# Seven block products in place of eight in the first feed-forward product, from the second quarter on

## The chip, the cores and the metric

The kernel runs on one core of one Trainium2 chip, in one launch. The metric is the device time of one execution in microseconds (us). A core has engines that each work through their own list of instructions in order and wait for each other by semaphores: TensorE (PE) for matrix products, VectorE (DVE) and ScalarE (ACT) for elementwise work, GpSimd (POOL), and SyncE (SP), which here only issues DMA transfers. Matrix products write to PSUM; everything else lives in SBUF. On TensorE each product is preceded by the load of its 128x128 stationary operand (PEld in the profile), which overlaps the product before it.

## The reference

One decoder layer on 256 tokens of width 2048, in float32. The part that matters here is the end of it, `x = x + merged @ w_out` and after that the feed-forward block:

```
def _rms(x, g):
    x32 = x.astype(jnp.float32)
    y = x32 * lax.rsqrt(jnp.mean(x32 * x32, axis=-1, keepdims=True) + EPS)
    return (y * g.astype(jnp.float32)).astype(x.dtype)
...
        h2 = _rms(x, g_ffn_norm[layer])
        x = x + jnp.square(jax.nn.relu(h2 @ w_ff_in[layer])) @ w_ff_out[layer]
```

`w_ff_in` is 2048 x 8192 and `w_ff_out` 8192 x 2048. Ahead of this lie three token mixers with their projections, gates and up-projections, which the change does not touch.

## The kernel before

**Products.** Every weight matrix is read from memory once, in float32, in tiles of two 128-row blocks by 512 columns (512 KB). Each tile lands in a buffer `raw` by a DMA that SP issues, is split by ACT into a rounded part `whi` (L159, L232) and by DVE into the rest `wlo` (L160, L233), and is used by TensorE for three products per 128-row block and token half: `whi` with the high and the low part of the activations, `wlo` with the high part. So a tile costs 2 token halves x 3 x 2 = 12 products of 512 columns. `wahead` (L200) keeps three tiles loaded and split ahead of the one in use; four buffers each hold `whi` and `wlo` (pool `wp`, L81), eight hold `raw` during the feed-forward block (pool `wff`, L700).

**Two ways to multiply.** `strip_rows` (L211) computes 256 tokens by 512 columns over 16 row blocks: 8 tiles, 96 products. `unit` (L238) computes 256 x 1024, that is two such strips. On the first four row blocks it treats the product as 2x2 blocks times 2x2 blocks and uses seven block products in place of eight, each with 6 matmuls: `B11`, `T2`, `T3`, `T1`, `B21`, `T4`, `B22`. The sums of weight blocks (`T1` to `T4`) are made by DVE in `uload` (L165) from four raw tiles that are loaded together, the sums of activation blocks by `sums_of` (L707, tiles `sf` and `ss`). The other 12 tiles of a unit are plain, marked `n`. A list of names, `UNIT`, says in which order products and plain tiles follow. Four of the block products go to PSUM tiles of their own (`pp`), and once they are done `early` adds them up on DVE (`uu`, `wz`) into what each output tile still lacks; `late` adds the accumulators `acc` at the unit's end.

**The feed-forward block.** It runs in four quarters (`for q in range(4)`, L741) of 2048 hidden columns. A quarter is four strips of `w_ff_in` with `strip_rows`, whose results are multiplied by the row scale of the norm (`ss2`, an ACT operand), put through relu and square (L724, L725), transposed by TensorE (L733) and split (`hid`), and then two units of `w_ff_out`. The norm's row scale is applied to the result of the first product, not to its input: the transposed activations `x1T` hold x times the gain alone. DVE and POOL compute `ss2` (L693 to L695).

**What sets the order.** The program is written as a loop over tiles. After each tile `pump` (L116) takes one step of pending work (transposes, splits, sums) from the queue `posts`, and one from `attn`. A scheduler then orders each engine's list from this program; the lists are fixed before the run.

Of the kernel before, what the change touches and what calls it, by code (L numbers as in the profile page):

```python
# [18 lines left out]
P = 128  # L19
# [21 lines left out]
GA = 2  # L41


UNIT = ["B11", "T2", "n", "T3", "n", "T1", "n", "B21", "n", "T4", "n", "B22", "n", "n", "n", "n", "n", "n", "n"]
UNIT_BLOCKS = [(0, 0), (1, 1), (0, 1), (1, 0)] + [(kg, c) for kg in range(2, KT // GA) for c in range(2)]


# [29 lines left out]
def tile_block(ctx: ExitStack, tc: tile.TileContext, io):  # L77
# [52 lines left out]
    for c in range(4):  # L130
        for name, nk in (("w_up_a", AH), ("w_up_b", BH), ("w_up_c", CH)):
            plan.extend([(name, GA, 512)] * (nk // GA))
        plan.extend([("w_gate", GA, 512)] * (min(3, 8 - 3 * c) * KT // GA))
    plan.extend([("w_out", GA, 512)] * (4 * KT // GA))
    for q in range(4):
        plan.extend([("w_ff_in", GA, 512)] * (4 * KT // GA))
        for _ in range(2):
            plan.extend((("w_ff_out", k) if k != "n" else ("w_ff_out", GA, 512)) for k in UNIT)
    offs = {}
    last_load = [None]  # L140
    pool = [wp]
# [534 lines left out]
    for c in range(4):  # L676
        acc = strip_rows("w_out", 512, KT, mh, ml)
        cs = slice(c * 512, (c + 1) * 512)
        for t in range(2):
            nc.vector.tensor_tensor(x1[:, t, cs], acc[t], x1[:, t, cs], op=ALU.add)  # L680
            sq = ff.tile([P, 512], F32, tag="sq2", name="sq2", bufs=2)
            nc.scalar.activation(sq, x1[:, t, cs], AF.Square, accum_out=stat2[:, t, c:c + 1])
        for j in range(2):
            tp = ps_tp.tile([P, 2, S], F32, tag="tp", name="tp")
            for i in range(2):
                kt = 4 * c + 2 * j + i
                for t in range(2):
                    nc.tensor.transpose(tp[:, i, t * P:(t + 1) * P], x1[:, t, kt * P:(kt + 1) * P], ident)  # L688
            for i in range(2):
                kt = 4 * c + 2 * j + i  # L690
                split_into(x1T[:, kt, 0, :], x1T[:, kt, 1, :], tp[:, i, :], vcol(V_FFN + kt))
# [12 lines left out]

    S_USE = {"T1": 0, "T2": 1, "T3": 2, "B22": 3}

    def sums_of(tps, ss):  # L707

        (a11, a12), (a21, a22) = [[tp[:, 2 * i:2 * i + 2, :] for i in range(2)] for tp in tps]
# [9 lines left out]
    def hidden_post(acc, hh, ss):  # L719

        ys = []
        for t in range(2):
            y = ff.tile([P, 512], F32, tag="y", name="y", bufs=4)
            nc.scalar.activation(y, acc[t], AF.Relu, scale=ss2[:, t:t + 1])  # L724
            nc.scalar.activation(y, y, AF.Square)  # L725
            ys.append(y)
        yield
        tps = []
        for t in range(2):
            yield  # L730
            tp = ps_tp.tile([P, 4, P], F32, tag="tp", name="tp")
            for i in range(4):
                nc.tensor.transpose(tp[:, i, :], ys[t][:, i * P:(i + 1) * P], ident)  # L733
            ts = slice(t * P, (t + 1) * P)
            split_into(hh[:, :, 0, ts], hh[:, :, 1, ts], tp)
            tps.append(tp)
        if ss is not None:
            yield
            sums_of(tps, ss)

    for q in range(4):  # L741
        hid = []
        for sidx in range(4):
            if sidx == 1:
                pool[0] = wff
            acc = strip_rows("w_ff_in", 512, KT, x1h, x1l)
            hh = ff.tile([P, 4, 2, S], F32R, tag="hid", name="hid", bufs=5)
            if sidx == 0:
                ss = ff.tile([P, 2, 4, 2, P], F32R, tag="ss", name="ss", bufs=1)
            gen = hidden_post(acc, hh, ss if sidx == 0 else None)  # L750
            next(gen)
            posts.append(("h", gen))
            hid.append(hh)
        hidh = lambda kt, t: hid[kt // 4][:, kt % 4, 0, t * P:(t + 1) * P]
        hidl = lambda kt, t: hid[kt // 4][:, kt % 4, 1, t * P:(t + 1) * P]
        h0 = hid[0]
        sums = {k: (lambda hl, g, i=i: ss[:, hl, i, g, :]) for k, i in S_USE.items()}
        sums["B11"] = lambda hl, g: h0[:, g, hl, 0:P]
        sums["B21"] = lambda hl, g: h0[:, GA + g, hl, 0:P]
        sums["T4"] = lambda hl, g: h0[:, GA + g, hl, P:S]  # L760
        for u in range(2):
            cols = [slice(1024 * u + 512 * c, 1024 * u + 512 * (c + 1)) for c in range(2)]

            def early(p1, p6, p7, p5):
                uu = ff.tile([P, 2, 512], F32, tag="uu", name="uu", bufs=1)
                wz = ff.tile([P, 2, 512], F32, tag="wz", name="wz", bufs=1)
                nc.scalar.copy(uu[:, 0, :], p1)
                nc.vector.tensor_tensor(x1[:, 0, cols[0]], p1, x1[:, 0, cols[0]], op=ALU.add)
                nc.vector.tensor_tensor(uu[:, 0, :], p6, uu[:, 0, :], op=ALU.add)
                nc.vector.tensor_tensor(uu[:, 1, :], p7, uu[:, 0, :], op=ALU.add)  # L770
                nc.vector.tensor_tensor(wz, p5[:, None, :].to_broadcast([P, 2, 512]), uu, op=ALU.add)
                nc.vector.tensor_tensor(x1[:, 1, cols[0]], uu[:, 1, :], x1[:, 1, cols[0]], op=ALU.add)
# [7 lines left out]
            unit("w_ff_out", sums, hidh, hidl, early, late)  # L780


def _consts():
# [62 lines left out]
```

## Time and profile before

| | |
|---|---|
| time, median of 3 runs | 1416.14 us (1415.92 to 1416.81) |
| the profiled execution's own time | 1416.98 us |
| its span | 1415.2 us |
| PE busy | 1405.5 us, 99% of the span |
| PEld busy | 1163.8 us, 82% |
| DVE busy | 890.1 us, 63% |
| ACT busy | 709.6 us, 50% |
| POOL busy | 36.6 us, 3% |
| memory read | 271.31 MB, 193 GB/s over the span |

The span runs from the first to the last instruction that the profiler saw; 1.78 us of the profiled execution's own time lie outside it. PE's busy time counts a product from its start to its modelled end, and products overlap: what a product costs in a row of products is the distance of their starts, which is total time by count.

### The profile page before, as it was taken

The numbers are of one execution on the slowest core, as the hardware profiler recorded it, in microseconds if no ns is written. First come the engines' busy times: TensorE is split into PE (matmuls) and PEld (weight loads), VectorE is DVE, ScalarE is ACT, GpSimd is POOL, SyncE is SP. The second block draws the span as 40 slices with busy tenths as digits, with TensorE's granted clock in tenths as the row PEclk, the third lists the DMA queues.
The fourth block names the chain that finished last, engine by engine and source line by source line (L and its number), as shares of the span: only waits on it lengthen the run. The fifth ranks groups of instructions, "written<-read, shape, count | busy, mean of one in ns | idle before, by whom it ended". The sixth has DMA issues, their size and how long they took to land.

```text
span 1415.2 us, 17005 instructions
## 1 busy us (share of the span) xinstructions
PE 1405.5 (99%) x6408; PEld 1163.8 (82%) x6408; DVE 890.1 (63%) x987; ACT 709.6 (50%) x881; POOL 36.6 (3%) x41
## 2 busy tenths in 40 slices
PE   8999999999999999999999999999999999999998
PEld 6888888888888888888888888888888888888887
DVE  6647657556655646565555786557865578655785
ACT  7545545465444444445455544455444554455542
POOL 0211102000000000000000000000000000000000
PEclk9999999999999999999999999999999999999999
DMA  9747545655566666676666557664676645766562
GB/s 320 238 143 238 169 149 164 200 180 169 185 202 200 196 201 207 193 241 191 185 247 184 155 184 248 189 186 149 195 240 190 185 155 194 239 185 187 155 229 92
DMA packets 79265, 274.51 MB, mean 194 GB/s; under 512 B 9040, under 2 KB 9808, under 8 KB 78928
## 3 DMA queue, kind: packets, MB, share of 16 engines
q1 hardware_dynamic: 79040, 273.42, 61.7%
q8 instruction: 50, 0.82, 0.2%
q14 instruction: 31, 0.25, 0.0%
q10 hardware_dynamic: 144, 0.02, 0.0%
HBM read 271.31 MB, written 2.10 MB: 193 GB/s over the span
## 4 chain that ended last, share of the span: by engine, by line
PE 74%; DVE 0%; issue 0%
PE acc L222 48%; PE acc L256 21%; PE pp L256 3%; PE tp L733 1%; PE tp L660 0%; PE tp L688 0%; DVE x L776 0%
## 5 line engine op out<-in xcount | busy, mean ns | idle before, releaser
L160 DVE TENSOR_TENSOR wlo<-raw,whi 128x1024 fp32r<-128x1024 f32 (+2 forms) x471 | 568.1, 1208 | 423.5 <-ACT whi L159 419.7
L159 ACT CAST whi<-raw 128x1024 fp32r<-128x1024 f32 (+2 forms) x471 | 489.2, 1040 | 576.8 <-PE acc L222 392.5
L222 PE MATMUL acc<-whi,xT 128*128 128x512 f32 (+1 forms) x1472 | 394.1, 389 | 5.3 <-ACT xT L235 5.3
L222 PEld LDWEIGHTS acc<-whi,xT 128*128 128x128 f32 x1472 | 273.1, 189 | 60.8 <-ACT xT L235 6.0
L222 PE MATMUL acc<-whi,x1T 128*128 128x512 f32 x1024 | 277.3, 392 | 0.0
L222 PE MATMUL acc<-wlo,xT 128*128 128x512 f32 (+1 forms) x736 | 227.1, 389 | 0.0
L256 PE MATMUL acc<-whi,hid 128*128 128x512 f32 x832 | 222.3, 390 | 0.0
L222 PEld LDWEIGHTS acc<-whi,x1T 128*128 128x128 f32 x1024 | 190.4, 188 | 38.6
L256 PEld LDWEIGHTS acc<-whi,hid 128*128 128x128 f32 x832 | 155.9, 188 | 32.4
L222 PEld LDWEIGHTS acc<-wlo,xT 128*128 128x128 f32 x736 | 137.3, 189 | 28.4 <-issue 1.0
L222 PE MATMUL acc<-wlo,x1T 128*128 128x512 f32 x512 | 157.8, 389 | 0.0
L256 PE MATMUL acc<-wlo,hid 128*128 128x512 f32 x416 | 125.3, 390 | 0.0
L222 PEld LDWEIGHTS acc<-wlo,x1T 128*128 128x128 f32 x512 | 96.1, 188 | 20.5
L256 PEld LDWEIGHTS acc<-wlo,hid 128*128 128x128 f32 x416 | 77.8, 188 | 16.0
L233 DVE TENSOR_TENSOR wlo<-raw,whi 128x1024 fp32r<-128x1024 f32 x56 | 68.3, 1220 | 27.0 <-ACT whi L232 21.3
L232 ACT CAST whi<-raw 128x1024 fp32r<-128x1024 f32 x56 | 58.9, 1053 | 45.1 <-PE acc L256 26.3
L222 PE MATMUL acc<-whi,mT 128*128 128x512 f32 x256 | 69.9, 391 | 0.0
L222 PE MATMUL acc<-whi,oT 128*128 128x512 f32 x224 | 60.0, 390 | 0.6 <-ACT oT L235 0.6
L222 PEld LDWEIGHTS acc<-whi,mT 128*128 128x128 f32 x256 | 47.8, 188 | 9.6
L222 PEld LDWEIGHTS acc<-whi,oT 128*128 128x128 f32 x224 | 42.0, 188 | 9.6 <-ACT oT L235 0.9
L222 PE MATMUL acc<-wlo,mT 128*128 128x512 f32 x128 | 40.0, 391 | 0.0
L222 PE MATMUL acc<-wlo,oT 128*128 128x512 f32 x112 | 34.8, 390 | 0.0
(160 smaller groups left out, 811.5 us busy)
## 6 DMA issues: line engine op xcount, KB each, us to landing
raw<-in_w_ff_in_dram SPq DMA_DIRECT2D x128, 512.0 KB, 3.9
raw<-in_w_ff_out_dram SPq DMA_DIRECT2D x128, 512.0 KB, 4.2
raw<-in_w_gate_dram SPq DMA_DIRECT2D x96, 512.0 KB, 3.6
raw<-in_w_proj_dram SPq DMA_DIRECT2D x77, 512.0 KB, 3.8
raw<-in_w_out_dram SPq DMA_DIRECT2D x32, 512.0 KB, 3.6
raw<-in_w_up_c_dram SPq DMA_DIRECT2D x12, 512.0 KB, 3.5
raw<-in_w_up_a_dram SPq DMA_DIRECT2D x8, 512.0 KB, 3.5
raw<-in_w_up_b_dram SPq DMA_DIRECT2D x8, 512.0 KB, 3.5
```

What stands on the lines that cost most here:

```text
L159: nc.scalar.copy(hi[:, gs, :], raw[:, gs, :])
L160: nc.vector.tensor_tensor(lo[:, gs, :], raw[:, gs, :], hi[:, gs, :].bitcast(F32), op=ALU.subtract)
L222: nc.tensor.matmul(acc[t][:, :n], lhsT=xs(kt, t), rhs=ws[:, g, :], start=(first and kt == 0), stop=(last and kt == nkt - 1),)
L232: nc.scalar.copy(hi, src)
L233: nc.vector.tensor_tensor(lo, src, hi.bitcast(F32), op=ALU.subtract)
L256: nc.tensor.matmul(acc, lhsT=x(hl, g), rhs=w[:, g, :], start=(first and i == 0 and g == 0), stop=(last and i == 2 and g == GA - 1))
L733: nc.tensor.transpose(tp[:, i, :], ys[t][:, i * P:(i + 1) * P], ident)
```

## The change

From the second quarter on, `w_ff_in` is multiplied by `unit` too: two units in place of four strips. The first quarter keeps its strips.

- The relu of a unit's result has no accumulator to read at once, since the block products must be added first. `late` now adds on DVE (L814 of the new code) into `y`, and relu and square run on ACT without a scale.
- So the scale must be in the activations. `scale_rows` spreads the row scale over a 128 x 256 tile `rrow` with two float32 products of a matrix of ones with a diagonal matrix `dg`, then rebuilds the activations in float32 (`xs`, four tiles of 128x1024 in the old weight buffers) and multiplies them by `rrow`. This runs on the side of the first quarter's strips.
- `split_rows` splits `xs` back into `x1T` when the first quarter's strips are done with it, and makes the activation sums for the block products (`sx`) once for all six new units.
- The list `UNIT` has two plain tiles more between `T2` and `T3`, and two fewer at its end, for old and new units alike.
- `early` and `partial_sums`: the copy of the first block product gets a tile of its own (`p1s`). `sq2` shares the buffers of `y`. The buffer reserved for software DMA descriptors is made smaller. The host's layout of `w_ff_in` follows the units.

```diff
-UNIT = ["B11", "T2", "n", "T3", "n", "T1", "n", "B21", "n", "T4", "n", "B22", "n", "n", "n", "n", "n", "n", "n"]
+UNIT = ["B11", "T2", "n", "n", "n", "T3", "n", "T1", "n", "B21", "n", "T4", "n", "B22", "n", "n", "n", "n", "n"]
...
+    def scale_rows():
+        tp = ps_sc.tile([P, S], F32, tag="sc", name="rr")
+        for t in range(2):
+            dg = ff.tile([P, P], F32, tag="a21", name="dg", bufs=1)
+            nc.vector.tensor_scalar(dg, ident, ss2[:, t:t + 1], None, op0=ALU.mult)
+            nc.tensor.matmul(tp[:, t * P:(t + 1) * P], lhsT=tri[:, P:], rhs=dg, start=True, stop=True)
+        nc.scalar.copy(rrow, tp)
+        for g in range(0, KT, 4):
+            yield
+            f = wp.tile([P, 4, S], F32, tag="raw", name="xs")
+            nc.vector.tensor_tensor(f, x1T[:, g:g + 4, 0, :].bitcast(F32), x1T[:, g:g + 4, 1, :].bitcast(F32),
+                                    op=ALU.add)
+            yield
+            nc.vector.tensor_tensor(f, f, rrow[:, None, :].to_broadcast([P, 4, S]), op=ALU.mult)
+            scaled.append(f)
+
+    def split_rows():
+        yield
+        for g, f in enumerate(scaled):
+            yield
+            split_into(x1T[:, 4 * g:4 * g + 4, 0, :], x1T[:, 4 * g:4 * g + 4, 1, :], f)
+            if g == 0:
+                yield
+                sums_of([[f[:, 2 * j:2 * j + 2, i * P:(i + 1) * P] for j in range(2)] for i in range(2)], sx)
...
-        for sidx in range(4):
+        for sidx in range(4 if q == 0 else 0):
             if sidx == 1:
                 pool[0] = wff
+                attn.append(("x", scale_rows()))
             acc = strip_rows("w_ff_in", 512, KT, x1h, x1l)
...
+        for u in range(2 if q else 0):
+            more = {}
+
+            def early(*p):
+                more[0, 0], more[0, 1], wz = partial_sums(*p)
+                more[1, 0], more[1, 1] = wz[:, 0, :], wz[:, 1, :]
+
+            def late(c, t, acc):
+                y = ff.tile([P, 512], F32, tag="y", name="y", bufs=4)
+                nc.vector.tensor_tensor(y, acc, more[c, t], op=ALU.add)
+                nc.scalar.activation(y, y, AF.Relu)
+                nc.scalar.activation(y, y, AF.Square)
+                more["y", t] = y
+                if t:
+                    first = u == 0 and c == 0
+                    posts.append(("h", hidden_rows([more["y", 0], y], hid[2 * u + c], ss if first else None,
+                                                   0 if c else 2)))
+
+            unit("w_ff_in", sums_for(lambda kt, hl, ts: x1T[:, kt, hl, ts], sx), x1h, x1l, early, late)
+        if q == 0:
+            drain(attn, "x")
+            attn.append(("x", split_rows()))
```

What this does to the engines' lists shows at three places. The first is TensorE in the second quarter's `w_ff_in`, where a strip had one kind of row: `acc` from `x1T`, here with the transposes of an earlier strip's `y` between.

```order
L222 MATMUL acc<-whi,x1T 128x512 x4
L222 MATMUL acc<-wlo,x1T 128x512 x2
L733 MATMUL tp<-ident,y 128x128 x4
L222 MATMUL acc<-whi,x1T 128x512 x4
L222 MATMUL acc<-wlo,x1T 128x512 x2
```

Now a new unit (its second in the quarter) begins with two block products of six matmuls each, `B11` from `x1T` and `T2` from the sums `sx`, and the transposes of the unit before follow at once.

```order
L262 MATMUL pp<-whi,x1T 128x512 x4
L262 MATMUL pp<-wlo,x1T 128x512 x2
L262 MATMUL pp<-whi,sx 128x512 x4
L262 MATMUL pp<-wlo,sx 128x512 x2
L262 MATMUL acc<-whi,x1T 128x512 x4
L752 MATMUL tp<-ident,y 128x128 x4
L262 MATMUL acc<-wlo,x1T 128x512 x2
```

The kinds of rows are those that a `w_ff_out` unit had before, with other operands.

The second place is VectorE at the head of that same new unit. There the splits of the coming weights (`wlo`) now stand between the splits of `hid` and the sums `sf` and `ss`.

```order
L738 TENSOR_TENSOR uu<-pp,p1s 128x512
L239 TENSOR_TENSOR wlo<-raw,whi 128x1024
L239 TENSOR_TENSOR hid<-tp,hid 128x4x128
L166 TENSOR_TENSOR wlo<-raw,whi 128x1024
L239 TENSOR_TENSOR hid<-tp,hid 128x4x128
L239 TENSOR_TENSOR wlo<-raw,whi 128x1024
L719 TENSOR_TENSOR sf<-tp,a21s 128x256
L720 TENSOR_TENSOR sf<-tp,a21s 128x256
L721 SCALAR_TENSOR_TENSOR sf<-tp,sf 128x256
L722 TENSOR_TENSOR sf<-tp,sf 128x256
L166 TENSOR_TENSOR wlo<-raw,whi 128x1024
L239 TENSOR_TENSOR ss<-sf,ss 128x1024
```

Before, the same sums stood among the splits of a strip, as here in the second quarter, where nothing else is pending.

```order
L233 TENSOR_TENSOR hid<-tp,hid 128x4x128
L160 TENSOR_TENSOR wlo<-raw,whi 128x1024
L233 TENSOR_TENSOR hid<-tp,hid 128x4x128
L713 TENSOR_TENSOR sf<-tp,a21s 128x256
L714 TENSOR_TENSOR sf<-tp,a21s 128x256
L715 SCALAR_TENSOR_TENSOR sf<-tp,sf 128x256
L160 TENSOR_TENSOR wlo<-raw,whi 128x1024
L716 TENSOR_TENSOR sf<-tp,sf 128x256
L160 TENSOR_TENSOR wlo<-raw,whi 128x1024
L233 TENSOR_TENSOR ss<-sf,ss 128x1024
```

So the sums moved from a strip, with one split per plain tile, into a unit, whose block products need a split every six matmuls.

The third place is VectorE in the first and second strip of the first quarter. Here are the rows of the change, from the first `xs` on; before, there were only `wlo` rows.

```order
L775 TENSOR_TENSOR xs<-x1T 128x1024
L166 TENSOR_TENSOR wlo<-raw,whi 128x1024
L775 TENSOR_TENSOR xs<-x1T 128x1024
L166 TENSOR_TENSOR wlo<-raw,whi 128x1024 x2
L775 TENSOR_TENSOR xs<-x1T 128x1024
L769 TENSOR_SCALAR dg<-ident,ss_95 128x128
L166 TENSOR_TENSOR wlo<-raw,whi 128x1024 x3
L778 TENSOR_TENSOR xs<-xs,rrow 128x1024 x4
L166 TENSOR_TENSOR wlo<-raw,whi 128x1024
L239 TENSOR_TENSOR hid<-tp,hid 128x4x128
```

The second `dg` stands behind the last `xs` addition, and the four multiplications by `rrow` stand in one piece between two weight splits.

On TensorE the second product from `dg` stands in the middle of the second strip's third tile, so TensorE's list holds there until `dg` is written.

```order
L228 MATMUL acc<-whi,x1T 128x512 x4
L770 MATMUL rr<-dg,tri 128x128
L228 MATMUL acc<-wlo,x1T 128x512 x2
```

Before, the two `L228` rows followed each other without it.

## Rows read from the trace of the kernel before

**Rows 1.** The page's busy time of each engine: us, share of span, instructions.

```profile
PE 1405.5 (99%) x6408; PEld 1163.8 (82%) x6408; DVE 890.1 (63%) x987; ACT 709.6 (50%) x881; POOL 36.6 (3%) x41
```

**Rows 2.** Whole run, whom PE waited for: us in total, times, longest us.

```profile
PE acc L222 <- ACT xT L235: 5.3, 2, 4.9
PE acc L222 <- ACT oT L235: 0.6, 1, 0.6
```

**Rows 3.** Chain of waits, second quarter: start us, us, what, count.

```profile
885.39 27.20 PE acc L222 x120
912.59 0.44 PE tp L733 x4
913.03 2.78 PE acc L222 x12
...
975.40 2.72 PE pp L256 x12
...
991.35 27.20 PE acc L256 x120
1018.55 2.72 PE pp L256 x12
...
1060.71 0.45 PE acc L222 x2
```

**Rows 4.** Busy us (and count) of PE, PEld, DVE, ACT, POOL by stretch; clock, DMA share, GB/s.

```profile
800.07:843.23 43.16, 43.16 (x196) 35.70 (x195) 34.19 (x34) 22.51 (x26) 0.00 (x0) 1.00 0.62 195
843.23:885.39 42.16, 42.16 (x188) 34.91 (x187) 30.31 (x30) 20.43 (x21) 0.00 (x0) 1.00 0.74 237
885.39:975.40 90.01, 90.01 (x410) 74.42 (x409) 50.62 (x48) 45.99 (x55) 0.00 (x0) 1.00 0.56 170
885.39:1060.71 175.32, 175.32 (x790) 145.03 (x789) 115.13 (x111) 88.92 (x99) 0.00 (x0) 1.00 0.62 192
```

**Rows 5.** PE timeline at float32 products of 128 columns: start us, us, what, records.

```profile
197.13 0.39 PE L564 MATMUL pn<-tri,nfb 128*128 128x128 f32 x2
197.35 0.60 PE L563 MATMUL pn<-tri,nfb 128*128 128x256 f32 x2
```

**Rows 6.** DVE timeline, head of the first quarter's second unit.

```profile
841.99 1.21 DVE L160 TENSOR_TENSOR wlo<-raw,whi 128x1024 fp32r<-128x1024 f32 x1
843.12 1.28 DVE L776 TENSOR_TENSOR x<-acc,x 128x512 f32<-128x512 f32 x2
844.32 1.22 DVE L233 TENSOR_TENSOR wlo<-raw,whi 128x1024 fp32r<-128x1024 f32 x1
845.45 1.22 DVE L160 TENSOR_TENSOR wlo<-raw,whi 128x1024 fp32r<-128x1024 f32 x1
```

**Rows 7.** PE timeline, the same head.

```profile
847.60 1.07 PE L256 MATMUL acc<-wlo,hid 128*128 128x512 f32 x4
...
850.10 0.62 PE L256 MATMUL pp<-wlo,ss 128*128 128x512 f32 x2
...
851.46 0.62 PE L256 MATMUL acc<-wlo,hid 128*128 128x512 f32 x2
```

**Rows 8.** DVE groups by form from 798 us on: count, busy us, mean ns, idle before, releaser.

```profile
L233 DVE TENSOR_TENSOR hid<-tp,hid 128x512 fp32r<-128x512 f32 x26 | 17.8, 683 | 0.0
L181 DVE TENSOR_TENSOR raw<-raw 128x1024 f32<-128x1024 f32 x7 | 8.6, 1226 | 8.1 <-DMA raw<-in_w_ff_out_dram 8.1
...
L714 DVE TENSOR_TENSOR sf<-tp,a21s 128x256 f32<-128x256 f32 x3 | 1.2, 415 | 0.0
```

**Rows 9.** Loads of plain tiles (L156) from 720 us on: us from issue to landing.

```profile
DMA to landing us min/median/max: 3.3/4.1/5.3
```

**Rows 10.** POOL and DVE timelines, end of the norm and the first two strips.

```profile
711.59 0.69 POOL L695 TENSOR_TENSOR ss<-ss,expo 128x2 f32<-128x2 f32 x1
...
712.59 1.22 DVE L160 TENSOR_TENSOR wlo<-raw,whi 128x1024 fp32r<-128x1024 f32 x1 [1.37 <-ACT whi L159]
...
727.81 3.62 DVE L160 TENSOR_TENSOR wlo<-raw,whi 128x1024 fp32r<-128x1024 f32 x3 [3.75 <-ACT whi L159]
```

**Rows 11.** ACT timeline: relu of the first strip's result, and a weight cast.

```profile
730.56 0.69 ACT L724 ACTIVATE y<-acc,ss 128x512 f32<-128x512 f32 x1 [0.58 <-PE acc L222]
...
734.13 1.05 ACT L159 CAST whi<-raw 128x1024 fp32r<-128x1024 f32 x1
```

More of the change, by code (lines that the diff above doesn't have):

```diff
@@ L134, in tile_block, with plan_units @@
     plan.extend([("w_out", GA, 512)] * (4 * KT // GA))
+    def plan_units(name):
+        for _ in range(2):
+            plan.extend((name, GA, 512) if k == "n" else (name, k) for k in UNIT)
     for q in range(4):
-        plan.extend([("w_ff_in", GA, 512)] * (4 * KT // GA))
-        for _ in range(2):
-            plan.extend((("w_ff_out", k) if k != "n" else ("w_ff_out", GA, 512)) for k in UNIT)
+        if q == 0:
+            plan.extend([("w_ff_in", GA, 512)] * (4 * KT // GA))
+        else:
+            plan_units("w_ff_in")
+        plan_units("w_ff_out")
     offs = {}
@@ L680, in tile_block @@
             nc.vector.tensor_tensor(x1[:, t, cs], acc[t], x1[:, t, cs], op=ALU.add)
-            sq = ff.tile([P, 512], F32, tag="sq2", name="sq2", bufs=2)
+            sq = ff.tile([P, 512], F32, tag="y", name="sq2", bufs=4)
             nc.scalar.activation(sq, x1[:, t, cs], AF.Square, accum_out=stat2[:, t, c:c + 1])
@@ L705, in tile_block, with sums_of @@
     S_USE = {"T1": 0, "T2": 1, "T3": 2, "B22": 3}
-    def sums_of(tps, ss):
-        (a11, a12), (a21, a22) = [[tp[:, 2 * i:2 * i + 2, :] for i in range(2)] for tp in tps]
+    def sums_of(a, ss):
+        (a11, a12), (a21, a22) = a
         sf = ff.tile([P, 4, 2, P], F32, tag="sf", name="sf", bufs=1)
@@ L717, in sums_of, with sums_for, partial_sums, hidden_rows @@
         split_into(ss[:, 0], ss[:, 1], sf)
[L719 to L727, printed above, removed]
+    def sums_for(at, ss):
+        sums = {k: (lambda hl, g, i=i: ss[:, hl, i, g, :]) for k, i in S_USE.items()}
+        sums["B11"] = lambda hl, g: at(g, hl, slice(0, P))
+        sums["B21"] = lambda hl, g: at(GA + g, hl, slice(0, P))
+        sums["T4"] = lambda hl, g: at(GA + g, hl, slice(P, S))
+        return sums
+    def partial_sums(p1, p6, p7, p5):
+        p1s = ff.tile([P, 512], F32, tag="p1", name="p1s", bufs=1)
+        uu = ff.tile([P, 2, 512], F32, tag="uu", name="uu", bufs=1)
+        wz = ff.tile([P, 2, 512], F32, tag="wz", name="wz", bufs=1)
+        nc.scalar.copy(p1s, p1)
+        nc.vector.tensor_tensor(uu[:, 0, :], p6, p1s, op=ALU.add)
+        nc.vector.tensor_tensor(uu[:, 1, :], p7, uu[:, 0, :], op=ALU.add)
+        nc.vector.tensor_tensor(wz, p5[:, None, :].to_broadcast([P, 2, 512]), uu, op=ALU.add)
+        return p1s, uu[:, 1, :], wz
+    def hidden_rows(ys, hh, ss, wait):
+        for _ in range(wait):
+            yield
         tps = []
@@ L738, in hidden_post @@
             yield
-            sums_of(tps, ss)
+            sums_of([[tp[:, 2 * i:2 * i + 2, :] for i in range(2)] for tp in tps], ss)
+    rrow = ff.tile([P, S], F32, name="rrow")
+    sx = ff.tile([P, 2, 4, 2, P], F32R, name="sx")
+    scaled = []
+    def scale_rows():
[13 more added lines that the diff above has]
+            scaled.append(f)
@@ L741, in tile_block @@
+    def split_rows():
[4 more added lines that the diff above has]
+            if g == 0:
+                yield
+                sums_of([[f[:, 2 * j:2 * j + 2, i * P:(i + 1) * P] for j in range(2)] for i in range(2)], sx)
     for q in range(4):
-        hid = []
-        for sidx in range(4):
+        hid = [ff.tile([P, 4, 2, S], F32R, tag="hid", name="hid", bufs=5) for _ in range(4)]
+        ss = ff.tile([P, 2, 4, 2, P], F32R, tag="ss", name="ss", bufs=1)
+        for sidx in range(4 if q == 0 else 0):
@@ L744, in tile_block @@
             if sidx == 1:
                 pool[0] = wff
+                attn.append(("x", scale_rows()))
             acc = strip_rows("w_ff_in", 512, KT, x1h, x1l)
[L747 to L753, printed above, removed]
+            ys = []
@@ new lines, in tile_block @@
+            for t in range(2):
+                y = ff.tile([P, 512], F32, tag="y", name="y", bufs=4)
+                nc.scalar.activation(y, acc[t], AF.Relu, scale=ss2[:, t:t + 1])
+                nc.scalar.activation(y, y, AF.Square)
+                ys.append(y)
+            posts.append(("h", hidden_rows(ys, hid[sidx], ss if sidx == 0 else None, 1)))
+        for u in range(2 if q else 0):
[4 more added lines that the diff above has]
+            def late(c, t, acc):
+                y = ff.tile([P, 512], F32, tag="y", name="y", bufs=4)
+                nc.vector.tensor_tensor(y, acc, more[c, t], op=ALU.add)
+                nc.scalar.activation(y, y, AF.Relu)
+                nc.scalar.activation(y, y, AF.Square)
+                more["y", t] = y
[4 more added lines that the diff above has]
+            unit("w_ff_in", sums_for(lambda kt, hl, ts: x1T[:, kt, hl, ts], sx), x1h, x1l, early, late)
@@ L754, in tile_block @@
+        if q == 0:
+            drain(attn, "x")
+            attn.append(("x", split_rows()))
         hidh = lambda kt, t: hid[kt // 4][:, kt % 4, 0, t * P:(t + 1) * P]
         hidl = lambda kt, t: hid[kt // 4][:, kt % 4, 1, t * P:(t + 1) * P]
[L756 to L760, printed above, removed]
@@ L761, in tile_block, with early @@
         for u in range(2):
             cols = [slice(1024 * u + 512 * c, 1024 * u + 512 * (c + 1)) for c in range(2)]
[L764 to L772, printed above, removed]
+            def early(*p):
+                p1s, u3, wz = partial_sums(*p)
+                nc.vector.tensor_tensor(x1[:, 0, cols[0]], p1s, x1[:, 0, cols[0]], op=ALU.add)
+                nc.vector.tensor_tensor(x1[:, 1, cols[0]], u3, x1[:, 1, cols[0]], op=ALU.add)
@@ L778, in late @@
                     load(io["out"][t * P:(t + 1) * P, cols[c]], x1[:, t, cols[c]])
-            unit("w_ff_out", sums, hidh, hidl, early, late)
+            unit("w_ff_out", sums_for(lambda kt, hl, ts: hid[0][:, kt, hl, ts], ss), hidh, hidl, early, late)
+        drain(attn, "x")
 def _consts():
@@ L833 @@
         "w_out": _blocked(a["w_out"][0], COL_STRIPS, GA),
-        "w_ff_in": _blocked(a["w_ff_in"][0], [[(c, 512)] for c in range(0, DFF, 512)], GA),
+        "w_ff_in": np.concatenate(
+            [_blocked(a["w_ff_in"][0][:, :DM], COL_STRIPS, GA), _units(a["w_ff_in"][0][:, DM:])]),
         "w_ff_out": np.concatenate([_units(a["w_ff_out"][0][q * DM:(q + 1) * DM]) for q in range(4)]),
     }
-    nc = _bacc.Bacc("TRN2", target_bir_lowering=False, num_devices=1)
+    nc = _bacc.Bacc("TRN2", target_bir_lowering=False, num_devices=1, dynamic_dma_scratch_size=4096)
     io = {}
```

## The prediction

> **What bounds the kernel now.** I read the page's busy times first: PE 99%, DVE 63%, ACT 50% [rows 1]. A busy share alone says nothing of a bound, so the waits of PE come next: two releasers in the whole run, 5.9 us together, both of activations (`xT`, `oT`) from long before the feed-forward block [rows 2]. So in the block PE never waits. The chain of waits agrees: through the second quarter it is PE, piece after piece, from a strip (885.39) over the first unit (975.40) and the second (1018.55) to the next quarter (1060.71) [rows 3]. The stretches then say how much room the others have: over that quarter DVE is busy 115.13 of 175.32 us, ACT 88.92, the clock stands at 1.00 (2.4 GHz), the DMA engines at 0.62 [rows 4]. A product taken from PE is worth its time there, as long as nothing that feeds PE becomes late.
>
> **Term 1, products removed: -8.16 us.** A strip has 8 tiles of 12 products, four strips 384. A unit has 7 block products of 6 and 12 plain tiles of 12, 42 + 144 = 186, two units 372. So a quarter loses 12 and three quarters lose 36. What one is worth: 120 in a row take 27.20 us in a strip and 27.20 us in a unit, 0.2267 us each [rows 3]. The price holds for block products too: the second unit is 42.16 us [rows 4], which is 186 x 0.2267 exactly, with its mixture of `pp` and `acc`. 36 x 0.2267 = 8.16. The Trainium skill (TensorE: Matmul & The Clock Gate, Back-to-back issue gap) gives about 131 ns for a product of 512 columns in a sustained stream; by that the 36 are worth 4.7 us and the time would end near 1412. This trace disagrees: 227 ns for the same form, measured at the very products that go; so I give that no chance of its own.
>
> **Term 2, products added: +0.5 us.** Two float32 products of 128 columns for `rrow`. The nearest rows are float32 products of the same size, which appear as two records each: two records from 197.13, the next form at 197.35 [rows 5], so 0.22 us a product, 0.44 for two. A switch costs a little: the 12 products behind four transposes take 2.78 instead of 2.72 us [rows 3]. That makes 0.5; the bounds are 0.2 (partly hidden) and 1.1 (four records end to end at 0.27). The transposes of `y` are as many as before.
>
> **Term 3, a wait for the second of these: 0.** It holds PE's list in the middle of the second strip's third tile. The strip begins where the relu of the first strip could start, about 730.5 [rows 11]; 28 products later it is 736.9. Before `dg` DVE has to do three weight splits, which end at 731.43 [rows 10], two `xs` additions at 1.13 (the distance of equal rows from 844.32 to 845.45) [rows 6] and `dg` itself: about 734. A lead of 2.9 us. The first `dg` needs `ss2`, ready at 712.28; DVE idles until 712.59 anyway [rows 10]. Bounds: 0, and 2 us once if the additions start late. Behind a late `dg` stand the next weight splits, and behind these PE. Then four multiplications in one piece hold DVE for 4 x 1.13 = 4.5 us; four `whi`/`wlo` buffers let the splits run about two tiles (5.4 us) ahead, so I take 0 here too, bound 1.
>
> **Term 4, VectorE in the new units: 0.** This decides. Per operation I take start distances: 1.13 us for 128x1024, 0.60 for 128x512 (two in 843.12 to 844.32) [rows 6], and for the small sums their 0.42 [rows 8]. The split of `hid` from PSUM, 683 ns long [rows 8], is of the 0.60 kind; so is the new `y` addition, which has the form of the old `x<-acc,x`.
>
> A unit needs 19 splits and 4 weight sums, 26.0 us. In the old units `early` adds 4.7 and `late` 2.4, and the first has two `hid` splits, 1.2: 31.9 + 33.1 = 65.0 for both. The rows show 34.19 + 30.31 = 64.5 [rows 4], so the count is good. Now the new `w_ff_in` units: `early` 2.3, `late` 2.4, and in the second four `hid` splits (2.4) and the sums (1.7 + 1.13 = 2.8): 35.9 us of 43.1. The first `w_ff_out` unit behind them: 26.0 + 4.7 + 2.4 + 2.4 = 35.5. In the first quarter it takes two to four of the 128x1024 splits of `xs` (two stand ahead of it): 34.2 to 36.4. All stay under 85%, where 79% ran without a wait [rows 4]. Over a quarter DVE gains 6 splits (6.8), 8 sums (9.0), partial sums (4.7) and additions (4.8): 115.1 + 25.3 = 140.4 of 172.6 us, 81%. In the mean there is room.
>
> The mean is not the danger; the head of a unit is, where block products want a split every 1.36 us. How far ahead is DVE there? At the old second unit's head the plain tile's split ends at 843.20 and is first used at 847.60, `T3`'s at 845.54 and 850.10, the next at 846.67 and 851.46 [rows 6, 7]: leads of 4.4, 4.6 and 4.8 us. Against that head the new second `w_ff_in` unit has 5.2 us more (`hid`, sums) and 2.4 less in `early`: 2.8. The first `w_ff_out` unit has 2.4 more, the first quarter's two to four splits. So the lead shrinks from 4.4 to 1.6 us at worst and PE does not wait. The two plain tiles moved up help: each gives DVE 2.72 us for 1.13 of work. If the cover were gone, a head would cost PE up to 2.8 us. Bounds: 0, and 7 heads (three of the one kind, four of the other) x 2.8 = 19.6.
>
> **Edits with no price.** ACT gains 6 casts and two copies a quarter, under 8 us on 88.92 of 175 [rows 4]; relu and square only change operands. The bytes are the same in 172.6 instead of 175.3 us. In a unit five of eight raw buffers hold blocks, now for two plain tiles longer. Three buffers remain: a load lands in at most 5.3 us [rows 9], cast and split take 1.05 [rows 11] and 1.22 [rows 6], so three tiles per 7.6 us, 2.5 each against the 2.72 that PE needs. That is thin, but it holds. `T3`'s sum waits for its third block in the old units (8.1 us in seven) [rows 8]; DVE has that room late in a unit, and will wait so in 14. The other units' `n` order, the shared `y` buffers and the descriptor buffer change nothing that PE waits for.
>
> **Sum.** -8.16 + 0.5 = -7.7. The profiled execution took 1416.98 with a span of 1415.2, so 1409.3 for an execution like it; the median of the runs lies 0.84 lower, so 1408.5.
>
> **Rivals.**
> 1. Short waits: at six or seven heads DVE or a load is late by about 0.5 us, since leads of 1.6 and buffers at 2.5 of 2.72 leave little. For it: `T3`'s wait for its block, up to seven times. Against it: the leads of 4.4 were measured with that wait in them. 7 x 0.5 = 3.5: 1412.
> 2. Slower: the splits lose the whole lead at those heads, because they stand in one list behind `hid` and the sums, which themselves wait for PE's transposes and ACT's casts; PE waits, so the transposes come later still. 19.6 us: 1428. It turns to a loss when a head costs over 7.7 / 7 = 1.1 us, which takes 2.7 us more DVE time there than I count. Against it: 81% over the quarter.
> 3. A wait once in the first quarter, for `dg` or behind the four multiplications: 1 to 3 us, 1409.5 to 1411.5.
> 4. The change does not shorten PE: what 36 products free goes back in denser switching (transposes between halves of a tile, `acc` left and resumed). For it: 0.06 us behind each group of transposes [rows 3]; to eat 7.7 it would take 128 more such switches, nine per unit. Then 1416. Against it: 42.16 in a unit that switches as much.
>
> **How the numbers follow.** The forecast (no new wait) 0.79, with its own range 1407.7 to 1409.3 from the bounds of term 2 and the spread of the runs; short waits 0.10; the first quarter's wait 0.04; denser switching 0.03; slower 0.04. Faster by over 0.2% (2.8 us, about what a measurement of this kernel tells from no change) hold the first three: 0.93, 0.03 same, 0.04 slower. The range 1407.4 to 1412 takes in the forecast, the first-quarter wait and most of the short waits.
>
> **What would show it.** Right: PE's waits still list only `xT` and `oT`; quarters two to four last 172.6 us each in the chain; a unit of 186 products lasts 42.2 us, plus 0.5 for each group of four transposes in it; DVE busy near 140 us a quarter. Wrong: PE waiting for DVE `wlo` in rows just behind `pp` products (rival 2 or 1), PE waiting for DVE `dg` near 737 (rival 3), or quarters longer than 173 us without any wait (rival 4). The prediction falls if DVE's new rows are longer than their forms in the old trace, or if a block's load lands later than 5.3 us in the middle of a unit.

## The result, and the profile after

| | before | after |
|---|---|---|
| time, median of the runs of this comparison | 1416.47 us (1415.92 to 1416.93) | 1408.73 us (1408.5 to 1409.0) |
| the profiled execution's own time, span | 1416.98, 1415.2 us | 1408.5, 1406.7 us |

The ratio is 0.9946, with a 95% interval from 0.9928 to 0.9963: 7.7 us faster. The forecast was 1408.5. Of the executions reported below one was slow, 1763.84 us at a granted clock of 0.753 (`e_new_list_only`); its ratio leaves it out.

The page's busy times of the kernel after, beside [rows 1]:

```profile
PE 1396.8 (99%) x6376; PEld 1157.6 (82%) x6376; DVE 980.6 (70%) x1090; ACT 732.3 (52%) x912; POOL 38.2 (3%) x41
```

DVE has 90.5 us more to do, PE 8.7 less. PE has 32 records fewer: 36 products of 512 columns went, and the two float32 products came with two records each. PE's share of the span is 99% as before, so what left PE left the time. Not all of the 8.7 us is the change's: a piece of 94 products ahead of the feed-forward block starts at 691.45 us in this execution and at 692.14 in the one before, so 0.7 us were gained ahead of it. Whom PE waited for in the whole run, the view of [rows 2]:

```profile
PE acc L228 <- ACT xT L241: 5.6, 2, 4.8
PE acc L228 <- ACT oT L241: 0.6, 1, 0.6
```

Only the two old waits are left, far ahead of the feed-forward block. The chain of waits through the second quarter, as in [rows 3] (start us, us, what, count):

```profile
885.18 2.72 PE pp L262 x12
887.91 8.16 PE acc L262 x36
...
927.35 2.72 PE pp L262 x12
...
971.47 2.72 PE pp L262 x12
...
1015.59 2.72 PE pp L262 x12
...
1057.75 2.72 PE pp L262 x12
```

Each `pp` piece with 12 products opens a unit (`B11`, `T2`). The quarter lasts from 885.18 to 1057.75, 172.57 us, where it lasted 175.32; `w_ff_in` takes 86.29 in place of 90.01. Of these 3.72 us, 2.72 are the 12 products; the other 1.0 are two groups of transposes that now stand in the units of `w_ff_out`, which take 86.28 in place of 85.31. The same four units as stretches, in the columns of [rows 4]:

```profile
885.18:927.35 42.17, 42.17 (x188) 34.95 (x187) 32.02 (x31) 22.06 (x24) 0.00 (x0) 1.00 0.63 200
927.35:971.47 44.12, 44.12 (x203) 36.50 (x203) 37.02 (x40) 27.78 (x35) 0.00 (x0) 1.00 0.62 191
971.47:1015.59 44.12, 44.12 (x204) 36.50 (x203) 36.59 (x38) 24.83 (x30) 0.00 (x0) 1.00 0.62 191
1015.59:1057.75 42.16, 42.16 (x188) 34.93 (x187) 34.19 (x34) 20.43 (x21) 0.00 (x0) 1.00 0.61 200
885.18:1057.75 172.57, 172.57 (x778) 142.89 (x777) 139.81 (x140) 95.10 (x107) 0.00 (x0) 1.00 0.62 195
```

PE is busy in every microsecond of each unit at full clock. DVE is busy 139.81 us of the quarter, and in its fullest unit, the second of `w_ff_in`, 37.02 of 44.12 (84%). The unit of 42.16 us holds 186 products, those of 44.12 the same and four groups of transposes at 0.44, with 0.05 for each switch.

The new work in the first quarter, from the chain of waits around the two products of `rrow`:

```profile
731.15 0.22 PE rr L770 x2
731.37 6.36 PE acc L228 x28
737.73 0.22 PE rr L770 x2
```

Each time two records, 0.22 us together, with the products going on before and behind. `dg` (the operation's durations in ns, first and last start):

```profile
L769 DVE TENSOR_SCALAR dg<-ident,ss x2: 284/286/288, 711.6 to 733.9; 128x128 f32<-128x128 f32 x2
```

The second was done at 734.2, 3.5 us before PE came to it at 737.7.

### The profile page after: what moved, and what is told of

The parts are those of the page before. It is cut to its first block, busy times and chain, and to the rows that moved or that the text cites. A ratio compares the mean times of both kernels' runs of the same rounds, so it can differ in the third digit from the quotient of the medians.

```text
span 1406.7 us, 17102 instructions
## 1 busy us (share of the span) xinstructions
PE 1396.8 (99%) x6376; PEld 1157.6 (82%) x6376; DVE 980.6 (70%) x1090; ACT 732.3 (52%) x912; POOL 38.2 (3%) x41
## 4 chain that ended last, share of the span: by engine, by line
PE 74%; DVE 0%; issue 0%
PE acc L262 37%; PE acc L228 30%; PE pp L262 5%; PE tp L752 1%; PE tp L694 0%; PE tp L666 0%; DVE x L839 0%; PE rr L770 0%
## 5 line engine op out<-in xcount | busy, mean ns | idle before, releaser
L166 DVE TENSOR_TENSOR wlo<-raw,whi 128x1024 fp32r<-128x1024 f32 (+2 forms) x447 | 536.4, 1206 | 301.0 <-ACT whi L165 296.4
L165 ACT CAST whi<-raw 128x1024 fp32r<-128x1024 f32 (+2 forms) x447 | 464.0, 1039 | 509.6 <-PE acc L228 290.4
L228 PE MATMUL acc<-whi,xT 128*128 128x512 f32 (+1 forms) x1472 | 393.8, 389 | 5.6 <-ACT xT L241 5.6
L228 PEld LDWEIGHTS acc<-whi,xT 128*128 128x128 f32 x1472 | 272.9, 189 | 60.8 <-ACT xT L241 6.3
L228 PE MATMUL acc<-wlo,xT 128*128 128x512 f32 (+1 forms) x736 | 226.6, 388 | 0.0
L262 PE MATMUL acc<-whi,x1T 128*128 128x512 f32 x624 | 169.0, 391 | 0.0
L228 PEld LDWEIGHTS acc<-wlo,xT 128*128 128x128 f32 x736 | 137.1, 188 | 28.1 <-issue 1.0
L238 ACT CAST whi<-raw 128x1024 fp32r<-128x1024 f32 x98 | 103.2, 1053 | 95.5 <-PE acc L262 78.3
L239 DVE TENSOR_TENSOR wlo<-raw,whi 128x1024 fp32r<-128x1024 f32 x98 | 119.8, 1223 | 42.6 <-ACT whi L238 38.2
L262 PEld LDWEIGHTS acc<-whi,x1T 128*128 128x128 f32 x624 | 116.8, 188 | 23.9
L262 PE MATMUL acc<-wlo,x1T 128*128 128x512 f32 x312 | 95.6, 391 | 0.0
L228 PE MATMUL acc<-whi,mT 128*128 128x512 f32 x256 | 70.0, 392 | 0.0
L228 PE MATMUL acc<-whi,x1T 128*128 128x512 f32 x256 | 69.8, 394 | 0.0
L262 PEld LDWEIGHTS acc<-wlo,x1T 128*128 128x128 f32 x312 | 58.4, 188 | 12.0
L228 PE MATMUL acc<-whi,oT 128*128 128x512 f32 x224 | 60.1, 390 | 0.6 <-ACT oT L241 0.6
L228 PEld LDWEIGHTS acc<-whi,mT 128*128 128x128 f32 x256 | 47.9, 188 | 9.6
L228 PEld LDWEIGHTS acc<-whi,x1T 128*128 128x128 f32 x256 | 47.5, 188 | 9.5
L228 PEld LDWEIGHTS acc<-whi,oT 128*128 128x128 f32 x224 | 42.0, 188 | 9.5 <-ACT oT L241 0.9
```

What stands on the lines that cost most here:

```text
L165: nc.scalar.copy(hi[:, gs, :], raw[:, gs, :])
L166: nc.vector.tensor_tensor(lo[:, gs, :], raw[:, gs, :], hi[:, gs, :].bitcast(F32), op=ALU.subtract)
L228: nc.tensor.matmul(acc[t][:, :n], lhsT=xs(kt, t), rhs=ws[:, g, :], start=(first and kt == 0), stop=(last and kt == nkt - 1),)
L262: nc.tensor.matmul(acc, lhsT=x(hl, g), rhs=w[:, g, :], start=(first and i == 0 and g == 0), stop=(last and i == 2 and g == GA - 1))
```

## The experiments

The runs fall into three questions: is the gain the products' price, what covers VectorE's new work, and what covers the loads. Each kernel is the changed one with the edit shown, if nothing else is said; times are medians, and ratios stand against the kernel before.

**A third of the products** (`e_q23`). The second quarter goes back to strips, from the scaled activations; 12 of the 36 products come back.

```diff
-        for sidx in range(4 if q == 0 else 0):
+        for sidx in range(4 if q < 2 else 0):
...
-                nc.scalar.activation(y, acc[t], AF.Relu, scale=ss2[:, t:t + 1])
+                nc.scalar.activation(y, acc[t], AF.Relu, scale=ss2[:, t:t + 1] if q == 0 else 1.0)
...
-        for u in range(2 if q else 0):
+        for u in range(2 if q > 1 else 0):
```

> The second quarter goes back to four strips (its activations carry the scale already, so its relu has none); only the third and fourth quarter multiply by units. Theory A (the gain is the number of products taken from PE, 0.2267 us each): 12 products come back, 2.72 us, so 1408.7 + 2.7 = 1411.4. Rival (a product is worth 131 ns): 12 x 0.131 = 1.6, 1410.3. Rival (switching in the units eats part): less than 2 us back.

1411.78 us, ratio 0.9966 (0.9953 to 0.9978): 3.05 of the gain given back. The chain of waits over the same quarter:

```profile
886.24 29.92 PE acc L228 x132
...
976.26 2.72 PE pp L262 x12
...
1061.56 2.72 PE pp L262 x12
```

886.24 to 1061.56 is 175.32 us, as before the change, and 2.75 more than with units. For 12 products that is 0.229 us each; PE's waits are the same two. The Trainium skill's 131 ns for a product in a sustained stream (TensorE: Matmul & The Clock Gate, Back-to-back issue gap) would give, as an estimate, 12 x 0.131 = 1.57 us for the quarter; the chain disagrees with it.

**The scale left at the relu** (`e_relu_scale`). A positive row scale can be applied behind the sum. `scale_rows` and `split_rows` go; one addition rebuilds the four row blocks that the sums need.

```diff
-    def scale_rows():
...
-    def split_rows():
+    def x_sums():
+        f = wp.tile([P, 4, S], F32, tag="raw", name="xs")
+        nc.vector.tensor_tensor(f, x1T[:, 0:4, 0, :].bitcast(F32), x1T[:, 0:4, 1, :].bitcast(F32), op=ALU.add)
         yield
...
-                nc.scalar.activation(y, y, AF.Relu)
+                nc.scalar.activation(y, y, AF.Relu, scale=ss2[:, t:t + 1])
```

> The units of quarters two to four stay, but the activations are left unscaled: the row scale is an operand of the relu behind the addition, and the two float32 products, the eight scaling operations and the four new splits of the activations go; one addition of 128x1024 remains for the sums. Theory A: only term 2 comes back, 0.5 us, so 1408.2; VectorE's work in the first quarter was hidden. Rival (the scaling costs a wait in the first quarter): 1 to 3 us come back, 1405.7 to 1407.7.

1408.87 us, 0.9944 (0.9932 to 0.9957). The half microsecond is too small to be seen in the times (this median is 0.14 above the changed kernel's). It shows that nothing larger hides in the preparation, and that the scale need not be in the activations, as the account of the change had it. The first quarter's strips as one stretch (columns of [rows 4]), in the kernel after:

```profile
710.00:797.00 87.00, 87.00 (x403) 72.06 (x402) 63.59 (x68) 49.09 (x63) 0.89 (x2) 1.00 0.59 196
```

and in this one:

```profile
710.00:797.00 87.00, 87.00 (x401) 71.97 (x400) 53.38 (x57) 46.92 (x61) 0.89 (x2) 1.00 0.63 198
```

DVE has 10.2 us less to do there, PE is busy throughout either way, and the time is the same: this DVE work was hidden whole.

**The list of names** (`e_old_list`, and `e_new_list_only` for the kernel before with the new list).

```diff
-UNIT = ["B11", "T2", "n", "n", "n", "T3", "n", "T1", "n", "B21", "n", "T4", "n", "B22", "n", "n", "n", "n", "n"]
+UNIT = ["B11", "T2", "n", "T3", "n", "T1", "n", "B21", "n", "T4", "n", "B22", "n", "n", "n", "n", "n", "n", "n"]
```

> The change with the list of names as it was before: T3 comes two plain tiles earlier. Theory A (heads have a lead of 1.6 us, which the two tiles helped to by 2 x (2.72 - 1.13) = 3.2 us): the lead falls to -1.6, seven heads x 1.6 = 11 us, 1420. Rival (VectorE's room in the mean of a unit is the cover, and the list gives nothing): 1408.7.

> The kernel before with the new list of names alone, so it moves only the eight units of the second product. Theory A: nothing waited there, 1416.5 within 0.5. Rival (part of the gain is the list's): 1412 to 1415.

With the old list the change takes 1409.03 us, 0.9946 (0.9932 to 0.9959), and PE waits for nothing new; the new list alone is worth nothing, 1416.44 us, 0.9999 (0.9989 to 1.0009). So the list is not what makes the change work, and theory A, by which the heads need those two tiles, falls. What the list does move is the lead, the time from the end of a weight split on DVE to its first product. I counted it over all splits from 800 us on in both traces: the smallest is 3.09 us after, 2.04 with the old list. The 2.04 of the old list is the lead of the block product `B21` in the new second unit, here on DVE:

```profile
937.32 1.22 DVE L239 TENSOR_TENSOR wlo<-raw,whi 128x1024 fp32r<-128x1024 f32 x1 [0.42 <-ACT whi L238]
```

and on PE, where it ends at 938.54 and is used at 940.58:

```profile
940.58 0.62 PE L262 MATMUL acc<-wlo,x1T 128*128 128x512 f32 x2
```

**More VectorE work in every unit** (`e_dve2`, `e_dve5`, `e_dve6`, `e_dve7`, `e_dve8`). The addition for `wz` is written several times, to the same result; each repeat costs DVE 1.13 us per unit, with no wait of its own and nothing for any other engine.

```diff
-        nc.vector.tensor_tensor(wz, p5[:, None, :].to_broadcast([P, 2, 512]), uu, op=ALU.add)
+        for _ in range(6):
+            nc.vector.tensor_tensor(wz, p5[:, None, :].to_broadcast([P, 2, 512]), uu, op=ALU.add)
```

This is `e_dve5`; the number in a label is that of the repeats, one less than the range.

> The changed kernel with the addition into wz written three times instead of once in every unit: two more operations of 1.13 us on VectorE behind T1, the same result. Theory A (at seven heads the lead is 1.6 us): 2.27 - 1.6 = 0.7 us at each of seven, 1408.7 + 4.7 = 1413.4, with PE waiting for wlo behind the pp products. Rival B (the cover is a unit's mean room, 35.9 + 2.3 of 43 us): 1408.7.

> The same with five more such operations, 5.65 us a unit. Theory A: 4.05 us at seven heads and 1.25 us (against leads of 4.4) at the other seven, 37 us, 1446. Rival B: the busiest unit is at 35.9 + 5.7 = 41.6 of 43 us and still fits, 1408.7 to 1411.

> As the run with five more additions into wz per unit, with six: 6.8 us. The busiest unit of the changed kernel shows VectorE 37.02 of 44.12 us, so 7.1 us of room. Theory C (a unit's mean room is the cover, since the scheduler spreads the additions over the unit): 1408.7. Rival (room cannot be used up: part of it is waiting for casts and loads that no order fills): 1411 to 1425, with PE waiting.

> As above with seven: 7.9 us a unit. Theory C: 0.8 us too much in the two units of a quarter with 44.1 us, none in the others, 6 x 0.8 = 5 us: 1414. Rival: between the run with six and the one with eight (1452), 1425 to 1440.

> The same with eight more, 9.04 us a unit, 36.2 a quarter. Theory A: 7.4 us at seven heads and 4.6 at seven, 84 us, 1493. Rival B: 139.8 + 36.2 = 176.0 of 172.6 us a quarter, so VectorE is the bound by 3.4 us a quarter or a little more: 1419 to 1430.

| repeats | added per unit | time | ratio (95%) | PE's waits for DVE and ACT in units |
|---|---|---|---|---|
| 2 | 2.26 us | 1408.51 | 0.9941 (0.9926 to 0.9956) | none |
| 5 | 5.65 us | 1408.77 | 0.9943 (0.9928 to 0.9958) | none |
| 6 | 6.8 us | 1430.14 | 1.0094 (1.0079 to 1.011) | 13.2 us |
| 7 | 7.9 us | 1440.0 | 1.0166 (1.0152 to 1.0179) | 20.0 us |
| 8 | 9.04 us | 1452.2 | 1.0248 (1.0233 to 1.0263) | 28.3 us |

Five repeats cost nothing, and the theories that priced two and five from a head's lead fall with their 1413.4 and 1446. The last three units of the second quarter then look so (columns of [rows 4]; each stretch begins some 0.7 us ahead of the unit):

```profile
927.40:971.50 44.10, 44.10 (x204) 36.46 (x203) 39.38 (x42) 27.06 (x34) 0.00 (x0) 1.00 0.61 191
971.50:1015.60 44.10, 44.10 (x204) 36.45 (x203) 40.99 (x42) 25.70 (x31) 0.00 (x0) 1.00 0.61 191
1015.60:1057.80 42.20, 42.20 (x188) 34.96 (x187) 39.83 (x39) 20.35 (x21) 0.00 (x0) 1.00 0.63 200
```

DVE is busy 94% of the last of them and PE all of it. The smallest lead anywhere is down to 1.37 us and still no product is late. A sixth repeat costs 21 us. Whom PE waits for with six repeats:

```profile
PE acc L262 <- DVE y L815: 10.0, 3, 3.3
PE acc L228 <- ACT xT L241: 5.1, 2, 4.8
PE tp L753 <- DVE hid L239: 3.0, 3, 1.1
PE acc L228 <- ACT oT L241: 0.6, 1, 0.6
PE acc L262 <- DVE wlo L166: 0.2, 1, 0.2
```

It is not the weight splits (`wlo`, 0.2 us). It is operations that read a PSUM tile and so free it, three times, once a quarter near the start of the first `w_ff_out` unit: first a split of `hid`, which frees a tile for the transposes (3.0 us in all), then `y`, the additions of `late`, which free an accumulator for the next unit (10.0). With eight repeats the shares turn round, 15.8 us for `hid` and 7.2 for `y`. Where the last pair of `y` stands on DVE with five repeats:

```profile
970.17 1.22 DVE L741 TENSOR_TENSOR wz<-pp,uu 128x1024 f32<-128x1024 f32 x1
...
974.16 1.28 DVE L815 TENSOR_TENSOR y<-acc,wz 128x512 f32<-128x512 f32 x2
```

and with six:

```profile
975.77 1.21 DVE L741 TENSOR_TENSOR wz<-pp,uu 128x1024 f32<-128x1024 f32 x1
...
980.38 1.21 DVE L741 TENSOR_TENSOR wz<-pp,uu 128x1024 f32<-128x1024 f32 x1
...
983.78 1.28 DVE L815 TENSOR_TENSOR y<-acc,wz 128x512 f32<-128x512 f32 x2
```

One repeat more, and `y` is done 9.6 us later, because the repeats of the old unit are now spread among the splits of the next one and `y` needs the last of them. The room at this place was used up before the unit's total was: with five repeats DVE already has no idle time over 0.1 us from 952.55 to 984.65. That `y` is so late may belong to the choice of operation, since the repeats write `wz`, which this pair reads; no run repeats an operation on which nothing depends. PE at that place with six repeats (in brackets the idle time before a row):

```profile
980.51 0.66 PE L753 MATMUL tp<-ident,y 128*128 128x128 f32 x4 [0.92 <-DVE hid L239]
984.51 1.58 PE L262 MATMUL acc<-whi,hid 128*128 128x512 f32 x4 [3.34 <-DVE y L815]
...
986.74 1.91 PE L262 MATMUL acc<-whi,hid 128*128 128x512 f32 x4
...
990.35 1.08 PE L262 MATMUL acc<-whi,hid 128*128 128x512 f32 x4
```

The product waits until 984.51, when the first of the pair is done. The four behind it take 1.91 us where four take 1.08 a little later: the clock, to which I come back. With five and six repeats the spans are 1407.2 and 1428.3 us, PE's busy times 1397.5 and 1405.5, so the 21.1 us are 13.2 of waiting and 8.0 of slower products; with eight, 28.3 and 14.4 of 42.9. Of the expectations, the rival's range for seven (1425 to 1440) just reaches the time; for six the rival was the nearer and too low, and for eight both missed.

**Fewer raw buffers** (`e_raw7`, `e_raw6`).

```diff
-    wff = ctx.enter_context(tc.tile_pool(name="wff", bufs=8, side="right"))
+    wff = ctx.enter_context(tc.tile_pool(name="wff", bufs=7, side="right"))
```

> The changed kernel with seven raw buffers instead of eight in the feed-forward block. Theory A (five of them hold blocks for most of a unit, so two are left for plain tiles): a tile takes (4.1 + 1.05 + 1.22) / 2 = 3.2 us against 2.72, over some nine tiles a unit 4 us, in 14 units 60 us: 1469. Rival B (the blocks come free one after the other, and SP issues far enough ahead): 1408.7.

> The changed kernel with six raw buffers. With seven nothing was lost: casts waited 23 us in all for loads and PE never. Theory B (the split tiles ahead of PE, four whi and wlo, take up a late load, and the blocks come free one after the other): some of these waits now pass the lead of about 3 us, a few us in all, 1409 to 1420. Theory A (the count of free buffers sets the pace: one buffer left beside five blocks, 4.2 + 1.05 + 1.22 = 6.5 us a plain tile against 2.72 for about nine tiles a unit): 34 us a unit, over 1700.

Seven buffers: 1408.93 us, 0.9943 (0.9927 to 0.996), no loss. ACT's casts do wait for loads more often (its waits from 700 us on; with eight buffers they were 1.9 us for `w_ff_out` and 7.9 for `w_ff_in`):

```profile
ACT whi L165 <- DMA raw<-in_w_ff_out_dram: 17.0, 14, 3.3
...
ACT whi L165 <- DMA raw<-in_w_ff_in_dram: 13.9, 10, 2.9
```

PE did not notice, and theory A's 1469 falls. Six buffers: 1480.47 us, 1.046 (1.0443 to 1.0478). Whom PE waited for then:

```profile
PE acc L262 <- ACT whi L165: 51.3, 30, 3.0
```

Behind this stand ACT's own waits for loads, 96.2 us in 33 cases for `w_ff_out` and 67.2 in 28 for `w_ff_in`. So the loads have one buffer to spare, not two; both my numbers for six missed, one too high and one too low.

**Units in the first quarter too** (`e_q0_units`). `e_relu_scale` makes it possible: if the activations need no scale, a unit need not wait for the norm. The sums are made while `w_out` still runs, and the first unit begins with six plain tiles.

```diff
+UNIT0 = ["n"] * 6 + ["B11", "T2", "n", "T3", "n", "T1", "n", "B21", "n", "T4", "B22", "n", "n"]
...
+        plan_units("w_ff_in", UNIT0 if q == 0 else UNIT)
...
+        if c == 0:
+            attn.append(("x", x_sums()))
...
-        for sidx in range(4 if q == 0 else 0):
...
-        for u in range(2 if q else 0):
+        for u in range(2):
...
-                nc.scalar.activation(y, y, AF.Relu)
+                nc.scalar.activation(y, y, AF.Relu, scale=ss2[:, t:t + 1])
```

> All four quarters multiply by units, the row scale is an operand of the relu, and nothing scales the activations. The sums of the activations are made during the second strip of the product before (w_out), and the first unit of the first quarter takes six plain tiles ahead of its block products, since its raw buffers come free only when that product is done. Theory A (products taken from PE, as long as the splits keep a lead): 12 products more, 2.72, and the two float32 products, 0.5, go: 1408.7 - 3.2 = 1405.5. Rival (the block's start is late: five raw buffers at once, just freed): 1 to 3 us are lost there, 1406.5 to 1408.5, with PE waiting for whi or wlo between 710 and 760.

1406.08 us (1404.63 to 1406.59), 0.9923 (0.9911 to 0.9936): faster than both kernels. It is 2.65 us under the changed one; the ranges of their runs lie apart, the intervals of their ratios overlap a little. The time lies between theory A's 1405.5 and the rival's range, which begins at 1406.5; the waits decide. Its busy times on the page:

```profile
PE 1393.4 (99%) x6360; PEld 1153.8 (82%) x6360; DVE 991.1 (71%) x1105; ACT 736.6 (53%) x915; POOL 36.6 (3%) x41
```

PE has 16 records fewer than the changed kernel, 12 products and two float32 products of two records, and 3.4 us less busy time; 12 x 0.2267 + 0.44 is 3.2. PE's waits:

```profile
PE acc L228 <- ACT xT L241: 4.9, 1, 4.9
PE acc L228 <- ACT oT L241: 0.6, 1, 0.6
```

So the rival's wait at the block's start is not there: the block products found their sums ready.

## Why the prediction was right, and where its working was not

**Term 1 (-8.16): right, and shown twice.** The quarter in units lasts the forecast 172.6 us (172.57 for the second and, from 1057.75 to 1230.32, for the third), and the quarter turned back gives 2.75 of it back. Rival 4, that denser switching eats the gain, would have shown as a quarter near 175 without waits; it isn't there.

**Term 2 (+0.5): 0.44**, two products of 0.22. The sum of the two terms, -7.7, is what the medians differ by (1416.47 - 1408.73 = 7.74). That is closer than the executions agree among themselves (1415.92 to 1416.93 before, 1408.5 to 1409.0 after), so the last tenths are luck. No run could show 0.44 us in the time itself.

**Term 3 (0): right.** `dg` was done at 734.2 (forecast 734) and used at 737.7 (forecast 736.9). The 10.2 us of DVE work taken out in `e_relu_scale` moved nothing. Rival 3 didn't occur.

**Term 4 (0): the quarter's count and the conclusion right, the argument at the heads wrong.** DVE's quarter has 139.81 us, forecast 140.4. The sums of single units were 1.1 us too low each (35.9, 35.5 and 33.1 against 37.02, 36.59 and 34.19), probably because an operation with idle time behind it takes 1.22 us and not the 1.13 of a start distance. The check on the old units does not hold as written: its 31.9 leaves out the first unit's `late`, and with it the two make 67.4, not 65.0, against 64.5 in the rows. Neither slip changes a conclusion, since PE did not wait. The argument at the heads does fail. I let all the new work of a unit fall on the head's lead, so that 4.4 us would shrink to 1.6. The lists spread this work over the unit instead: at the new second unit's head the first plain tile's split ends at 927.27 and is used at 931.17, a lead of 3.9. The shortest lead of that unit comes later, at the block product `B21`, whose split on DVE

```profile
942.63 1.23 DVE L239 TENSOR_TENSOR wlo<-raw,whi 128x1024 fp32r<-128x1024 f32 x1 [0.40 <-ACT whi L238]
```

ends at 943.86 and is used on PE at

```profile
947.47 0.62 PE L262 MATMUL acc<-wlo,x1T 128*128 128x512 f32 x2
```

a lead of 3.6, even with 0.40 us in which DVE had nothing to do. Over the whole block the smallest lead went from 3.51 to 3.09 us. So the 0 came out for another reason than the one given. Four runs go against the weight splits at a head as the critical place: the old list costs nothing, nor do 2.26 or 5.65 us more per unit, and where it breaks, PE waits for `hid` and `y` and only 0.2 us for a split. So "it takes 2.7 us more DVE time there" as the turning point of rival 2 was too small. The cover lies between 5.65 and 6.8 us a unit, just under the room of the fullest one (44.1 - 37.0 = 7.1).

**"If the cover were gone, a head would cost up to 2.8 us": wrong in place and size.** With six repeats the late operations are those that free PSUM tiles (`hid`, then `y`), and PE then stands near the start of the next unit, three times in the run, at about 7 us a time (21.1 / 3, the clock's part in it).

**The raw buffers ("thin, but it holds"): held with more to spare than counted.** Three free buffers at 2.5 us a tile against 2.72 would make two too slow (3.8). Two were enough. Why two are, the runs do not settle: the shortage lasts for part of a unit only, and the prepared tiles may carry PE across it; I did not follow the buffers one by one. The loads of blocks landed after up to 5.4 us in the kernel after, just over the 5.3 us that the prediction named as a sign of its fall; DVE waited 20.0 us for them in all and PE never.

Rival 1, short waits at the heads, rested on the leads of 1.6 and on these buffers; neither was so.

## What to carry to other kernels

When one engine has no waits, price what leaves it by the distance of starts in a long uniform row, and test the price by giving back a known part of it. To find how much an engine beside it can still take, repeat one of its operations in steps: the answer here was nothing up to 94% of a unit and 21 us one step later, and what PE then waited for was not the feed everyone looks at but operations that give PSUM tiles back. Repeat more than one kind of operation, for the one that is repeated may choose what is late first; that was not tested here. A factor that is positive and constant over a row can stand behind the product and the sums: that removed a preparation here at no cost and opened the first quarter to the same saving.

## What the runs showed of the hardware that was not expected

A wait of PE cost more than itself here. Around the stall of 0.92 and 3.34 us shown above, in the kernel with six repeats (columns of [rows 4]; the figure behind POOL's is the granted clock):

```profile
980.00:984.00 4.00, 0.66 (x4) 0.42 (x4) 4.00 (x5) 0.58 (x1) 0.00 (x0) 1.00 0.82 255
984.00:988.00 4.00, 3.49 (x9) 2.78 (x10) 2.25 (x4) 2.27 (x4) 0.00 (x0) 0.64 0.75 247
988.00:992.00 4.00, 4.00 (x20) 3.27 (x19) 0.83 (x1) 1.58 (x2) 0.00 (x0) 0.93 0.01 2
992.00:996.00 4.00, 4.00 (x19) 3.29 (x19) 3.36 (x5) 2.46 (x4) 0.00 (x0) 1.00 0.48 137
```

PE was idle for most of the first 4 us; the clock granted in the next is 0.64, between its two levels of 2.4 and 1.2 GHz (1.00 and 0.50), and it is back at 1.00 from 992 on. Over the runs with repeats, PE's busy time grew by 8.0, 11.6 and 14.4 us over that with five while it waited 13.2, 20.0 and 28.3 us; with six raw buffers by 16.1 over the changed kernel's, for 51.0 us more of waiting. The granted clock is enough to account for the growth with repeats. Over their whole spans these three executions were granted 0.994, 0.990 and 0.989, where the one with five has 1.000; the missing shares are 8.6, 14.4 and 16.0 us, and some of that fell where PE stood idle. The three stalls are not alike: with six repeats the clock is 0.91 from 980 to 1000, and 0.83 both from 1160 to 1180 and from 1340 to 1360, which is 1.8, 3.4 and 3.4 us. With six raw buffers the whole span has 0.995, which is 7.4 us of the 16.1 at most; what the rest is stays open.
